# Half of a projection made early: the first layer's output product during the attention, for five token tiles instead of two

## The chip, the cores and the metric

The program runs on one core of a Trainium2 chip. The metric is the device time of one execution in microseconds (us), the median over runs. A core has a matrix engine (PE, with its weight loads shown as PEld), a vector engine (DVE), a scalar engine (ACT), a general engine (POOL) and a queue engine that issues the transfers (SP). Each engine takes its own instructions strictly in the order in which the program lists them, and waits at an instruction until what it needs is there.

## The reference, cut to what matters

The program is one inference step of a two-layer trunk over 640 token rows (512 latent rows and 128 prompt rows, five tiles of 128) of width 1024, in float32 accuracy. In the first layer one input projection feeds two kinds of heads, whose outputs stand side by side and go through one output projection:

```python
o_gla = rmsnorm(o_gla, g_gla) * jax.nn.silu(g_a.reshape(B, L, H_A, DV_A))      # 4 linear-attention heads: 512 columns
...
o_swa = banded_attn(q_b..., k_b, v_b, k_ctx, v_ctx, scale, sink_g)             # 8 windowed softmax heads: 512 columns
...
out = jnp.concatenate([o_gla.reshape(B, L, H_A * DV_A), o_swa.reshape(B, L, H_B * D_B)], axis=-1) @ w_out
```

Then, for each token row, `x = x + gate * rmsnorm(out, g)`, and the squared-ReLU network of the layer on `rmsnorm(x)` with a shift and a scale. The second layer (latent attention and a second network) is untouched here.

## The kernel before, in words

Every product keeps float32 accuracy by splitting each operand into a high and a low part: `mm3` (L136 to L140) issues three matmuls, high by high, high by low, low by high, into one accumulator. A weight tile of 128x1024 comes by DMA into one of three `raw` buffers; `split` casts its high part on ACT (L133) and subtracts on DVE (L134) into two tiles of the `ring`, which has 12 buffers (tag `w`, names `wt`, `q`, `kh`, `kl`, `Pr`, `PTr`).

The activations of all five tiles lie in `Hh` and `Hl` (high and low) as eight row blocks of 128. Blocks 0 to 3 are written by the linear attention (`gla_out`, L821), blocks 4 to 7 by the windowed softmax attention (`swa`, L932). The output projection of a tile is 8 blocks times 2 column halves times 3 matmuls, 48 matmuls of 128x512 into two accumulators `pso`.

The order of stages around the change is this. `gla_plan` finishes the products of the input projection and the linear attention. `swa` then runs eight heads for each of five tiles: `queries` transposes a tile's queries (`psq`) and splits them into `q`; `scores` copies the sink logit into the last column of a two-bank accumulator `pss` on ACT (L967) and makes the scores there (L970, L971, and the band mask L973); `soft_max` takes the row maximum on DVE (L979), `soft_exp` the exponential on ACT (L990), `soft_div` scales on POOL (L996); `trans` transposes the probabilities on PE (`pspt`, L1008) and copies them out as `PT` (L1009, by ACT and DVE in turn); `values` multiplies with the values into the accumulator `psov` (L1018), and `store` splits the result into `Hh` and `Hl`. `mod_steps` runs beside it: 96 matmuls `psmod` on 12 transfers of 1 MB (`mraw`), for the modulation vectors.

`out_ahead` (L497) makes blocks 0 to 3 of the output projection for the first `OA = 2` tiles while the attention runs, since these blocks are ready, and ACT copies each half into `acc` (L505). It gets the accumulator bank that the modulation holds until then; the other bank of that tag is `psov`. After the attention, `out_proj` (L508) makes blocks 4 to 7 for tiles 0 and 1 and adds to `acc` on DVE (L530), and all eight blocks for tiles 2 to 4 with a copy of the result (L532). `post` (L433) follows for each tile: a sum of squares on ACT (L309), two small POOL operations (L311, L312), a DVE scaling (L437), the residual add on POOL (on DVE for tile 4; L438) and its store; then `pre` (L319): again a sum of squares, the two POOL operations, a DVE scaling into `xn` (L324), eight transposes on PE (`pst`, L327), scale and shift by DVE and ACT (L335, L332), and the split into `Hh` (ACT, L339) and `Hl` (DVE L341, POOL through L130). `ff` (L536) starts with six feature blocks on tiles 0 and 1 ("part 0", matmuls `psf` of 128x256), then the same blocks on tiles 2 to 4 ("part 1", 128x384).

The code lists these steps in an order set by tables of planned times (`GLA_PLAN`, `SWA_PLAN`); a list scheduler then merges what it can for each engine by its own estimate of readiness and the priorities, so a change of the code can move instructions well away from the lines that it edits.

Of the kernel before, what the change touches and what calls it, by code (L numbers as in the profile page):

```python
# [11 lines left out]
F32 = mybir.dt.float32  # L12
# [31 lines left out]
OA = 2  # L44
# [52 lines left out]
def kernel(ctx: ExitStack, tc: tile.TileContext, I, O, dbg=None, stop=None):  # L97
# [390 lines left out]
    def out_weights(load, ks, alloc=None):  # L488
        wt = {}
        for k in ks:  # L490
            for n in range(2):
                hi, lo = wtile([P, 2, 512], lambda r: load(r, k, n), alloc if k == 6 else None)
                for i in range(2):
                    wt[k + i, n] = hi[:, i, :], lo[:, i, :]
        return wt

    def out_ahead(load, pp, acc, ts):  # L497

        wt = out_weights(load, (0, 2))
        for t in ts:  # L500
            for n in range(2):
# [3 lines left out]
                s.copy(out=acc[t][:, n * 512:(n + 1) * 512], in_=ps)  # L505
        return wt

    def out_proj(l, load, np_, pp, gate, accs, ahead=None):  # L508

        def alloc():  # L510
            return hid_tile(np_).rearrange("p a b -> p (a b)")

        begun = ()
        if ahead:
            wt, begun = ahead
        else:
            wt = out_weights(load, (0, 2))
        wt.update(out_weights(load, (4, 6), alloc))
        for t in range(NT):
            ts = slice(t * P, (t + 1) * P)  # L520
            pss = [pp.tile([P, 512], F32, tag="mm", name="pso") for _ in range(2)]
            k0 = 4 if t in begun else 0
            for k in range(k0, KD):
                for n in range(2):
                    mm3(pss[n], (Hh[:, k, ts], Hl[:, k, ts]), wt[k, n], k == k0, k == KD - 1)
            acc = begun[t] if k0 else accs(t)
            for n in range(2):
                c = slice(n * 512, n * 512 + 512)
                if k0:
                    v.tensor_tensor(out=acc[:, c], in0=pss[n], in1=acc[:, c], op=ALU.add)  # L530
# [62 lines left out]
    def mixer_ab(ap, bp, pa, pf, wf):  # L593
# [102 lines left out]
        qb = A["qb"] = bp.tile([P, NT, 512], F32, name="qb")  # L696
        gg = A["gg"] = ap.tile([P, NT, 512], F32, name="gg")
        ge = ap.tile([P, 512], F32, name="ge")
# [122 lines left out]
    def gla_out(A, p, pp, ap):  # L821
# [5 lines left out]
        for n0, nn in ((0, NS), (NS, 1)):  # L827
# [104 lines left out]
    def swa(A, pp, sp, ap, side):  # L932
# [29 lines left out]
        def scores(t, h):  # L962
# [4 lines left out]
            s.copy(out=ps[:, n:n + 1], in_=sink[:, h:h + 1])  # L967
            for o, k0, w in segs:
# [29 lines left out]
        def trans(t, kv, b):  # L998
# [5 lines left out]
            if (t, kv) not in EARLY:  # L1004
                PTs[t, kv][b] = sp.tile([P, 512], F32, tag="PT", name="PT", bufs=12)
# [486 lines left out]
    with pools(st=7, md=1) as ps:  # L1492
        with sb("start") as sp:
            pa, pf, wf = start(sp, ps)
        bp, ap = ms.enter_context(sb("bp")), gs.enter_context(sb("ap"))
        gp = gs.enter_context(sb("gp", "right"))
        A, products = mixer_ab(ap, bp, pa, pf, wf)
    with ms, pools(mm=2, gm=2, w2=2) as ps:
# [5 lines left out]
        def acc_tile(np_, t):  # L1504
            early = t < OA
            return (acp if early else np_).tile([P, D], F32, tag="acc", name="acc", bufs=OA if early else NT - OA)
        with sb("wa") as wa, sb("wp") as wp:
# [4 lines left out]
            begun = {t: acc_tile(None, t) for t in range(OA)}  # L1512
            ahead = out_ahead(load_w_out, ps, begun, range(OA)), begun
    with pools(mm=4, h=3, md=1) as ps:
        consts = mla_consts(dk, ps)
        with sb("fp") as fp:
            accs = lambda t: acc_tile(fp, t)
            out_proj(0, load_w_out, fp, ps, load_gate(0, 0, fp), accs, ahead)
# [3 lines left out]
            ff(0, fp, ps, lambda: load_gate(0, 1, fp), fp, accs,  # L1522
# [61 lines left out]
```

## Time and profile before

| what | value |
|---|---|
| runs | 1722.38, 1723.40 and 1726.54 us, median 1723.4 us |
| profiled execution | 1723.44 us, of which the span from first to last instruction is 1721.7 us |
| PE busy | 1652.6 us (96% of the span), mean granted clock 0.981 |
| DVE, ACT, POOL busy | 875.7, 682.4, 355.7 us |

The profiled execution lies 0.04 us from the median of the runs, and 1.7 us of it lie outside the span. In a list of instructions a row reads: start in us, length in us, engine, line, operation, output from inputs, shapes, count, and in brackets how long the engine stood idle before and what ended the wait. A PE row's length includes the drain of its pipeline, so back-to-back matmuls start closer together than their length.

### The profile page before, as it was taken

How to read it: one execution, taken by the hardware profiler on the slowest of the kernel's cores; microseconds unless marked ns; L12 is line 12 of the kernel's file. 1: busy time of each engine (PE TensorE's matmuls, PEld its weight loads, DVE VectorE, ACT ScalarE, POOL GpSimd, SP SyncE). 2: the span in 40 equal slices, each digit the busy share in tenths (PEclk: the TensorE clock that was granted, in tenths of full speed). 3: DMA queues.
4: the chain of work that ended last, by engine and by line, in shares of the span. 5: the costliest groups of instructions: out<-in, count | busy, mean ns of one | idle time of the engine just before them, and what ended most of it. 6: DMA issues, size and time to landing. Idle time of an engine off the chain costs nothing.

```text
span 1721.7 us, 25685 instructions
## 1 busy us (share of the span) xinstructions
PE 1652.6 (96%) x10270; PEld 1423.9 (83%) x10270; DVE 875.7 (51%) x1509; ACT 682.4 (40%) x1358; POOL 355.7 (21%) x422
## 2 busy tenths in 40 slices
PE   6989989999999999999999899999999999999997
PEld 5877775668998888889987788888889988999896
DVE  5368856546334343344476656566363344444443
ACT  4345345536341232132365565666353422232231
POOL 1135522233000000000163554443230000000003
PEclk9999989999999999999999999999999999999999
DMA  9311118156236465542231000112252321322212
GB/s 316 92 53 53 40 63 273 44 171 219 75 110 213 142 196 168 185 144 74 74 128 54 27 28 25 38 38 75 86 172 74 99 84 43 94 86 78 73 47 98
DMA packets 130933, 178.65 MB, mean 104 GB/s; under 512 B 7783, under 2 KB 95854, under 8 KB 129790
## 3 DMA queue, kind: packets, MB, share of 16 engines
q1 hardware_dynamic: 130814, 177.01, 32.6%
q8 instruction: 81, 1.33, 0.3%
q14 instruction: 38, 0.31, 0.1%
HBM read 165.93 MB, written 11.06 MB: 103 GB/s over the span
## 4 chain that ended last, share of the span: by engine, by line
PE 86%; DVE 6%; ACT 3%; DMA 2%; POOL 1%; issue 1%; SPq 0%; POOLq 0%; DVEq 0%; ACTq 0%
PE psf L138 9%; PE psf L139 9%; PE psf L140 9%; PE ps L138 8%; PE ps L139 8%; PE ps L140 8%; PE pso L1372 3%; PE psP L1350 3%; PE pso L138 2%; PE pso L139 2%; PE pso L140 2%; PE psmod L293 2%; PE pst L138 1%; PE psS L138 1%; PE psS L139 1%; PE psS L140 1%
## 5 line engine op out<-in xcount | busy, mean ns | idle before, releaser
L133 ACT CAST wt<-raw 128x1024 fp32r<-128x1024 f32 (+1 forms) x164 | 170.3, 1041 | 418.3 <-PE ps L139 240.7
L138 PE MATMUL psf<-Hh,wt 128*128 128x256 f32 (+1 forms) x1072 | 332.4, 311 | 1.2 <-ACT vt L656 1.2
L140 PE MATMUL psf<-Hh,wt 128*128 128x256 f32 (+1 forms) x1072 | 331.6, 309 | 0.0
L139 PE MATMUL psf<-Hl,wt 128*128 128x256 f32 (+1 forms) x1072 | 331.4, 309 | 0.0
L134 DVE TENSOR_TENSOR wt<-raw,wt 128x1024 fp32r<-128x1024 f32 (+1 forms) x164 | 207.4, 1267 | 224.7 <-ACT wt L133 206.5
L138 PE MATMUL ps<-wt,hid 128*128 128x512 f32 x640 | 250.3, 391 | 0.0
L139 PE MATMUL ps<-wt,hid 128*128 128x512 f32 x640 | 249.5, 390 | 0.0
L140 PE MATMUL ps<-wt,hid 128*128 128x512 f32 x640 | 249.2, 389 | 0.0
L138 PEld LDWEIGHTS psf<-Hh,wt 128*128 128x128 f32 x1072 | 203.3, 190 | 10.1 <-ACT hid L545 4.2
L311 POOL TENSOR_SCALAR ss<-ss 128x1 f32<-128x1 f32 x50 | 15.6, 312 | 943.8 <-ACT junk L309 943.1
L139 PEld LDWEIGHTS psf<-Hl,wt 128*128 128x128 f32 x1072 | 203.4, 190 | 1.4 <-issue 0.8
L140 PEld LDWEIGHTS psf<-Hh,wt 128*128 128x128 f32 x1072 | 203.5, 190 | 0.0
L583 DVE TENSOR_TENSOR acc<-ps,acc 128x512 f32<-128x512 f32 x120 | 82.3, 691 | 179.0 <-PE ps L140 178.9
L138 PEld LDWEIGHTS ps<-wt,hid 128*128 128x128 f32 x640 | 120.2, 188 | 32.0 <-ACT hid L545 4.2
L140 PEld LDWEIGHTS ps<-wt,hid 128*128 128x128 f32 x640 | 120.2, 188 | 25.0
L139 PEld LDWEIGHTS ps<-wt,hid 128*128 128x128 f32 x640 | 120.2, 188 | 24.3
L546 DVE TENSOR_TENSOR r<-r 128x384 f32<-128x384 f32 (+1 forms) x128 | 62.3, 488 | 110.0 <-ACT hid L545 109.9
L544 ACT ACTIVATE r<-psf 128x384 f32<-128x384 f32 (+1 forms) x128 | 55.6, 435 | 128.5 <-PE psf L140 128.5
L1339 POOL TENSOR_SCALAR Pm<-Pm,sm 128x768 f32<-128x768 f32 (+1 forms) x80 | 64.6, 810 | 117.9 <-DVE sm L1337 114.4
L1331 ACT ACTIVATE Pm<-psS,sm 128x768 f32<-128x768 f32 (+1 forms) x80 | 63.6, 796 | 26.8 <-PE psP L1350 15.8
L1319 DVE TENSOR_REDUCE sm<-psS 128x1 f32<-128x768 f32 x64 | 61.2, 956 | 21.4 <-PE psS L140 18.2
L1350 PE MATMUL psP<-ident,Pm 128*128 128x128 f32 x400 | 65.0, 280 | 0.0
(353 smaller groups left out, 3002.4 us busy)
## 6 DMA issues: line engine op xcount, KB each, us to landing
raw<-in_w_ff SPq DMA_DIRECT2D x128, 512.0 KB
mraw<-in_w_mod SPq DMA_DIRECT2D x60, 512.0 KB
mraw<-in_w_mod SPq DMA_DIRECT2D x18, 1024.0 KB
raw<-in_w_in_ab SPq DMA_DIRECT2D x16, 512.0 KB
xdr<-xt SPq DMA_DIRECT2D x15, 512.0 KB
xt<-xdr SPq DMA_DIRECT2D x15, 512.0 KB
xt<-in_x_sample SPq DMA_DIRECT2D x8, 512.0 KB
gate<-gdr SPq DMA_DIRECT2D x8, 512.0 KB
```

The lines of the kernel that those rows point to most:

```text
L133: s.copy(out=hi, in_=src)
L134: sub(out=lo, in0=src, in1=f32(hi), op=ALU.subtract)
L138: pe.matmul(out, lhsT=ah, rhs=bh, start=first, stop=False)
L139: pe.matmul(out, lhsT=ah, rhs=bl, start=False, stop=False)
L140: pe.matmul(out, lhsT=al, rhs=bh, start=False, stop=last)
L544: s.activation(out=r[:, 0:n], in_=ps, func=ACTF.Relu)
L546: v.tensor_tensor(out=r[:, 0:n], in0=r[:, 0:n], in1=r[:, 0:n], op=ALU.mult)
L583: v.tensor_tensor(out=acc[t][:, ns], in0=pss[n], in1=acc[t][:, ns], op=ALU.add)
L1319: v.tensor_reduce(out=st[:, 0, 0:1], in_=ps[:, 0:768], axis=AX.X, op=ALU.max, negate=True)
L1331: s.activation(out=Pm[:, c], in_=ps[:, c], func=ACTF.Exp, bias=st[:, 0, x:x + 1], accum_out=st[:, 1, x:x + 1])
L1339: g.tensor_scalar(Pm[:, c], Pm[:, c], st[:, 1, x:x + 1], 1.0, op0=ALU.mult, op1=ALU.mult)
L1350: pe.transpose(pt[:, (b - a) * P:(b - a + 1) * P], Pm[:, b * P:(b + 1) * P], ident)
```

## The change

All five tiles get blocks 0 to 3 of the output projection during the attention, one column half after the other: first the left halves of tiles 0 to 4, then the right halves. `out_proj` then makes only blocks 4 to 7, and adds to `acc` for every tile. The accumulators of tiles 2 to 4 take the buffers in which the queries of the attention lay (a pool `qa` of three buffers, each of which holds the queries of two tiles first), so the accumulator of tile 2 is free after the queries of tile 1 are transposed, that of tile 3 after tile 3's, that of tile 4 after tile 4's. Smaller edits come with it: the sink logit is copied into `pss` after the score matmuls instead of before; the gate of the linear attention is computed in place in `gg` (the scratch tile `ge` goes); `gla_out` takes its two heads in the order 1, 0 in some loops; `PT` has 11 buffers instead of 12; and the weights of blocks 6 and 7 lie in the ring instead of in `hid`.

```diff
-    def out_ahead(load, pp, acc, ts):
-
-        wt = out_weights(load, (0, 2))
-        for t in ts:
-            for n in range(2):
+    def out_ahead(load, pp, acc):
+
+        for n in range(2):
+            wt = out_weights(load, (0, 2), (n,))
+            for t in range(NT):
                 ps = pp.tile([P, 512], F32, tag="mm", name="pso")
                 for k in range(4):
                     mm3(ps, (Hh[:, k, t * P:(t + 1) * P], Hl[:, k, t * P:(t + 1) * P]), wt[k, n], k == 0, k == 3)
                 s.copy(out=acc[t][:, n * 512:(n + 1) * 512], in_=ps)
...
-        begun = ()
-        if ahead:
-            wt, begun = ahead
-        else:
-            wt = out_weights(load, (0, 2))
-        wt.update(out_weights(load, (4, 6), alloc))
+        k0, wt = (4, out_weights(load, (4, 6))) if begun else (0, {**out_weights(load, (0, 2)), **out_weights(load, (4, 6), alloc=alloc)})
...
-        qb = A["qb"] = bp.tile([P, NT, 512], F32, name="qb")
+        qbs = [qa.tile([P, D], F32, tag="qa", name="qb", bufs=3) for _ in range(3)]
+        qb = A["qb"] = [qbs[t // 2][:, t % 2 * 512:t % 2 * 512 + 512] for t in range(NT)]
...
             ps = pp.tile([P, 1024], F32, tag="w2", name="pss")
-            s.copy(out=ps[:, n:n + 1], in_=sink[:, h:h + 1])
             for o, k0, w in segs:
...
+            s.copy(out=ps[:, n:n + 1], in_=sink[:, h:h + 1])
...
-                PTs[t, kv][b] = sp.tile([P, 512], F32, tag="PT", name="PT", bufs=12)
+                PTs[t, kv][b] = sp.tile([P, 512], F32, tag="PT", name="PT", bufs=11)
...
-        def acc_tile(np_, t):
-            early = t < OA
-            return (acp if early else np_).tile([P, D], F32, tag="acc", name="acc", bufs=OA if early else NT - OA)
+        def acc_tile(t):
+            return acp.tile([P, D], F32, tag="acc", name="acc", bufs=2) if t < 2 else qa.tile([P, D], F32, tag="qa", name="acc", bufs=3)
...
-            begun = {t: acc_tile(None, t) for t in range(OA)}
-            ahead = out_ahead(load_w_out, ps, begun, range(OA)), begun
+            begun = [acc_tile(t) for t in range(NT)]
+            out_ahead(load_w_out, ps, begun)
```

No engine gets more or less work, but for six copies of `pso` to `acc` more on ACT during the attention, and six adds in place of six copies after it. What changes is the order. The line numbers of the change are lower than those of before: L504 there is L505 here, L966 is L967, L137 to L139 are L138 to L140.

The first place is ACT near the end of the attention (tile 4's queries `q`, the exponentials `Pm`, the stores `Hh` of the attention). Before:

```order
182 L505 COPY acc<-pso 128x512
183 L133 CAST Hh<-psov 128x4x128
184 L1009 COPY PT<-pspt 128x512
185 L959 ACTIVATE q<-psq 64x4x128
186 L990 ACTIVATE Pm,sm<-pss,sm 128x513
187 L1009 COPY PT<-pspt 128x512
188 L967 COPY pss<-sink 128x1
189 L959 ACTIVATE q<-psq 64x4x128
190 L967 COPY pss<-sink 128x1
191 L990 ACTIVATE Pm,sm<-pss,sm 128x513
192 L990 ACTIVATE Pm,sm<-pss,sm 128x129
```

With the change:

```order
177 L132 CAST Hh<-psov 128x4x128
178 L1002 COPY PT<-pspt 128x512
179 L966 COPY pss<-sink 128x1
180 L952 ACTIVATE q<-psq 64x4x128
181 L983 ACTIVATE Pm,sm<-pss,sm 128x513
182 L132 CAST wt<-raw 128x1024
183 L952 ACTIVATE q<-psq 64x4x128
184 L132 CAST wt<-raw 128x1024
185 L504 COPY acc<-pso 128x512
186 L1002 COPY PT<-pspt 128x512
187 L966 COPY pss<-sink 128x1 x2
188 L983 ACTIVATE Pm,sm<-pss,sm 128x513
```

Before, the row 182 is the last `acc` copy of the attention. With the change, four such copies stand before row 177 as before, and six more come from row 185 on, between exponentials, with two weight casts ahead of the first of them.

The second place is PE at the start of the windowed attention (`psq` the transposes of tile 0's queries, `pso` here the outputs of the linear attention, `pss` the scores). Before:

```order
704 L835 MATMUL pso<-va,AT 128x128 x4
705 L842 MATMUL pso<-sf_644,qh 128x128
706 L842 MATMUL pso<-st,qh 128x128 x6
707 L842 MATMUL pso<-sb_645,qh 128x128
708 L953 MATMUL psq<-ident,qb 128x128 x2
709 L835 MATMUL pso<-va,AT 128x128 x4
710 L842 MATMUL pso<-sf_644,qh 128x128
711 L842 MATMUL pso<-st,qh 128x128 x6
712 L842 MATMUL pso<-sb_645,qh 128x128
713 L953 MATMUL psq<-ident,qb 128x128 x2
714 L970 MATMUL pss<-kh,q 128x256
```

With the change:

```order
704 L946 MATMUL psq<-ident,qb 128x128 x4
705 L828 MATMUL pso<-va,AT 128x128 x4
706 L835 MATMUL pso<-sf_647,qh 128x128
707 L835 MATMUL pso<-st,qh 128x128 x6
708 L828 MATMUL pso<-va,AT 128x128 x4
709 L835 MATMUL pso<-sf_647,qh 128x128
710 L835 MATMUL pso<-st,qh 128x128 x6
711 L835 MATMUL pso<-sb_648,qh 128x128 x2
712 L962 MATMUL pss<-kh,q 128x256
```

The four transposes now stand ahead of the linear attention's outputs, and ACT makes `q` from them ahead of that attention's sums of squares; three heads of scores follow where one did.

The third place is ACT after the output projection (`junk` the sums of squares, of `acc` in `post` and of `xt` in `pre`; `r` and `hid` the results of the network's part 0). Before, from the sum of squares of tile 3's `acc`:

```order
223 L309 ACTIVATE junk,ss<-acc 128x1024
224 L133 CAST wt<-raw 128x1024 x3
225 L332 ACTIVATE hf<-pst,modT_85,gm_2801 128x128 x4
226 L309 ACTIVATE junk,ss<-xt 128x1024
227 L339 CAST Hh<-hf 128x4x128 x2
228 L133 CAST wt<-raw 128x1024 x2
229 L532 COPY acc<-pso 128x512
230 L309 ACTIVATE junk,ss<-acc 128x1024
```

With the change, from the same operation:

```order
222 L308 ACTIVATE junk,ss<-acc 128x1024
223 L132 CAST wt<-raw 128x1024
224 L331 ACTIVATE hf<-pst,modT_85,gm_2805 128x128 x4
225 L338 CAST Hh<-hf 128x4x128 x2
226 L536 ACTIVATE r<-psf 128x256
227 L537 ACTIVATE hid<-r 128x256
228 L536 ACTIVATE r<-psf 128x256
229 L537 ACTIVATE hid<-r 128x256
230 L308 ACTIVATE junk,ss<-xt 128x1024
231 L308 ACTIVATE junk,ss<-acc 128x1024
```

The sums of squares of tile 3's `xt` and of tile 4's `acc` now stand behind the results of the first two feature blocks of part 0. On PE the transposes `pst` of tile 4 stood among part 0 and now stand behind all of its 144 matmuls.

More of the change, by code (lines that the diff above doesn't have):

```diff
@@ L43 @@
 PVP = 150
-OA = 2
 QR = 1
@@ L486, in hid_tile, with out_weights @@
         return np_.tile([P, 2, T], R, tag="hid", name="hid", bufs=6)
-    def out_weights(load, ks, alloc=None):
+    def out_weights(load, ks, ns=(0, 1), alloc=None):
         wt = {}
         for k in ks:
-            for n in range(2):
+            for n in ns:
                 hi, lo = wtile([P, 2, 512], lambda r: load(r, k, n), alloc if k == 6 else None)
@@ L495, in out_weights @@
         return wt
-    def out_ahead(load, pp, acc, ts):
-        wt = out_weights(load, (0, 2))
-        for t in ts:
-            for n in range(2):
+    def out_ahead(load, pp, acc):
+        for n in range(2):
+            wt = out_weights(load, (0, 2), (n,))
+            for t in range(NT):
                 ps = pp.tile([P, 512], F32, tag="mm", name="pso")
@@ L505, in out_ahead, with out_proj @@
                 s.copy(out=acc[t][:, n * 512:(n + 1) * 512], in_=ps)
-        return wt
-    def out_proj(l, load, np_, pp, gate, accs, ahead=None):
+    def out_proj(l, load, np_, pp, gate, accs, begun=None):
         def alloc():
             return hid_tile(np_).rearrange("p a b -> p (a b)")
-        begun = ()
-        if ahead:
-            wt, begun = ahead
-        else:
-            wt = out_weights(load, (0, 2))
-        wt.update(out_weights(load, (4, 6), alloc))
+        k0, wt = (4, out_weights(load, (4, 6))) if begun else (0, {**out_weights(load, (0, 2)), **out_weights(load, (4, 6), alloc=alloc)})
         for t in range(NT):
@@ L590, in ff, with mixer_ab @@
             f0 += nf
-    def mixer_ab(ap, bp, pa, pf, wf):
+    def mixer_ab(ap, bp, qa, pa, pf, wf):
         w_in = I["w_in_ab"][0]
@@ L704, in use_q @@
             if t < NS:
-                rope_tok(qb[:, t, :], ps, t, 8, bp)
+                rope_tok(qb[t], ps, t, 8, bp)
             else:
-                s.copy(out=qb[:, t, :], in_=ps)
+                s.copy(out=qb[t], in_=ps)
         def use_g(t, ps):
+            ge = gg[:, t, :]
             s.activation(out=ge, in_=ps, func=ACTF.Exp, scale=-1.0)
@@ L712, in use_g @@
             s.activation(out=ge, in_=ge, func=ACTF.Exp, scale=-1.0)
-            v.tensor_tensor(out=gg[:, t, :], in0=ps, in1=ge, op=ALU.mult)
+            v.tensor_tensor(out=ge, in0=ps, in1=ge, op=ALU.mult)
         def use_b(a, c0, c1, ps, f=0):
@@ L833, in gla_out @@
             for n in range(n0, n0 + nn):
-                for r in range(2):
+                for r in ((1, 0) if nn > 1 else (0, 1)):
                     pe.matmul(ov(r, n), lhsT=AT[:, r, n, :], rhs=va[:, n, (2 * p + r) * P:(2 * p + r + 1) * P],
@@ L839, in gla_out @@
                 for d in range(2):
-                    for r in range(2):
+                    for r in (1, 0):
                         rs = slice(r * 64, r * 64 + 64)
@@ L952, in queries @@
             for x in range(4):
-                pe.transpose(ps[:, x, :], qb[:, t, x * P:(x + 1) * P], ident)
+                pe.transpose(ps[:, x, :], qb[t][:, x * P:(x + 1) * P], ident)
             q = (ring.tile([P, 1024], R, tag="w", name="q").rearrange("p (h n) -> p h n", h=HB) if t < QR
@@ L1516 @@
         with sb("fp") as fp:
-            accs = lambda t: acc_tile(fp, t)
-            out_proj(0, load_w_out, fp, ps, load_gate(0, 0, fp), accs, ahead)
+            out_proj(0, load_w_out, fp, ps, load_gate(0, 0, fp), acc_tile, begun)
             dump(h1h=f32(Hh), h1l=f32(Hl))
```

7 lines of the change are left out of this document (3 added, 4 removed).

## The prediction, made before the change was timed

> **What bounds the kernel now.** I read the page first, for the engine that bounds:
>
> ```profile
> span 1721.7 us, 25685 instructions
> PE 86%; DVE 6%; ACT 3%; DMA 2%; POOL 1%; issue 1%; SPq 0%; POOLq 0%; DVEq 0%; ACTq 0%
> ```
>
> 86% of the chain that ends last is PE, so a moved matmul gains nothing by itself: it must land where PE stood idle or slow. I then cut the stages around the change into windows (start and end, length, then busy time of PE, its weight loads, DVE, ACT, POOL, the clock granted to PE, the share of the transfers, GB/s):
>
> ```profile
> 220.00:230.00 10.00, 7.01 (x55) 6.25 (x53) 2.03 (x4) 4.62 (x21) 2.16 (x3) 0.89 0.03 8
> 307.90:329.60 21.70, 21.70 (x127) 16.24 (x126) 9.18 (x22) 9.21 (x27) 4.89 (x7) 1.00 0.10 25
> 329.60:354.60 25.00, 18.41 (x87) 10.69 (x87) 13.02 (x31) 11.87 (x39) 4.28 (x10) 0.78 0.15 43
> 354.60:403.00 48.40, 48.40 (x223) 40.15 (x224) 25.80 (x36) 24.02 (x43) 21.58 (x23) 0.97 0.51 168
> 403.00:423.40 20.40, 18.88 (x157) 18.47 (x156) 16.94 (x29) 13.21 (x29) 8.36 (x7) 1.00 0.88 297
> ```
>
> From 307.9 to 329.6 the four early units (12 matmuls each: one tile, one column half) fill PE completely. The 25.0 us behind them, the tail, hold nine heads (tile 3's last, tile 4's eight) with nothing to fill: PE is busy 18.41 us, at a clock of 0.78. Then come the output projection, 48.4 us of dense PE, and part 0 of the network, 20.4 us. The tail's lines, grouped, and its last rows on PE show what is late there:
>
> ```profile
> L1008 PE MATMUL pspt<-ident,Pm 128*128 128x128 f32 x36 | 8.0, 344 | 3.4 <-POOL Pm L996 2.1 <-DVE PT L1009 1.0
> L1018 PE MATMUL psov<-PT,vt 128*64 128x512 f32 x20 | 6.7, 811 | 0.8 <-DVE PT L1009 0.8
> ```
> ```profile
> 348.06 0.33 PE L970 MATMUL pss<-kh,q 128*128 128x128 f32 x1 [0.92 <-ACT pss L967]
> ...
> 351.32 0.48 PE L1008 MATMUL pspt<-ident,Pm 128*128 128x128 f32 x1 [1.53 <-POOL Pm L996]
> ...
> 352.58 1.98 PE L1018 MATMUL psov<-PT,vt 128*64 128x512 f32 x4 [0.78 <-DVE PT L1009]
> ```
>
> PE waits for the loop of a head: sink copy, maximum, exponential, division, transposes, copies. That is a wait which other matmuls can fill.
>
> **The change, part by part.**
>
> *Six units into the tail.* The price of a matmul is the distance of starts in a dense stretch:
>
> ```profile
> 358.81 0.39 PE L138 MATMUL pso<-wt,Hh 128*128 128x512 f32 x1
> ...
> 359.94 0.39 PE L140 MATMUL pso<-wt,Hl 128*128 128x512 f32 x1
> ...
> 417.19 1.09 PE L327 MATMUL pst<-ident,xn 128*128 128x128 f32 x8 [0.94 <-DVE xn L324]
> 418.04 0.37 PE L140 MATMUL psf<-Hh,wt 128*128 128x256 f32 x1
> 418.24 0.28 PE L138 MATMUL psf<-Hh,wt 128*128 128x256 f32 x1
> 418.36 0.28 PE L139 MATMUL psf<-Hl,wt 128*128 128x256 f32 x1
> ```
>
> The first two lie five starts apart: 1.13/5 = 0.226 us for 128x512. The last two give 0.12 us for 128x256; eight transposes take 418.04 − 417.19 = 0.85 us. The six moved units are 72 × 0.226 = 16.3 us. They leave the dense output projection, where they cost their full price. What they cost in the tail follows from the tail's own work at full clock. Upwards: 18.41 × 0.78 = 14.4 us, which counts drains as work. Downwards, by number: 36 transposes × 0.106 = 3.8, 20 of `psov` at 0.226 = 4.5, the remaining 18.41 − 8.0 − 6.7 = 3.7 us of scores and queries × 0.78 = 2.9; together 11.2. I take 13, so tail and units are 13 + 16.3 = 29.3 us of dense PE, more than the 25.0 that the heads' loop took. But the last head stands behind the last unit: from its score at 348.06 to 354.48 about 6.4 us passed, of which some 1.4 were matmuls; those 5 us of waits stay. The tail becomes 29.3 + 5 = **34 us**. The bounds are 29.3 (no wait left) and 25.0 + 16.3 = 41.3 (nothing filled). I lean to the side of the filled tail because of the window ahead of it: the same kind of unit, in the same one accumulator bank, held PE at 21.70 of 21.70 us. There a unit needs ACT's copy of the one before:
>
> ```profile
> 320.48 0.59 ACT L505 COPY acc<-pso 128x512 f32<-128x512 f32 x1 [1.33 <-PE pso L140]
> ```
>
> Six such copies more are 3.5 us on ACT, which is busy 11.87 of 25 us in the tail: beside PE, at nothing, unless a copy stands behind a blocked ACT (the slower rival).
>
> The Trainium skill speaks against this move: "TensorE: Matmul & The Clock Gate", section "A second HAM failure mode: psum-queue depth-cycling", says that a kernel which cycles accumulator banks leaves PE idle for short times between groups, so that its clock swings between half and full. By that the units would run at 0.78, as the tail does now, or less. The window 307.9 to 329.6 (clock 1.00, one bank, refilled four times) does not agree so far; the tail with units has no row here.
>
> *The way to part 1 on PE.* Part 1 begins with
>
> ```profile
> 423.26 0.52 PE L138 MATMUL psf<-Hh,wt 128*128 128x384 f32 x2
> ...
> 425.06 1.06 PE L293 MATMUL psmod<-mraw,cst 128*32 128x512 f32 x6
> ```
>
> and eight modulation matmuls (about 2 us) stand between its first; I count to 425.5. From 329.6 that is 25.0 + 48.4 + 20.4 + 2.1 = 95.9 us. With the change: 34 + 120 matmuls × 0.226 = 27.1, five tiles' transposes 4.3, part 0 of 144 × 0.12 = 17.2, modulation 2.1: 84.7 us, or **−11.2**. That assumes that the 3.9 us of holes which the stages now have beyond their count close; with them it would be −7.3.
>
> *The way to part 1 through ACT, DVE and POOL.* Behind the attention each tile needs two sums of squares on ACT with POOL and DVE steps between:
>
> ```profile
> 362.63 1.37 DVE L530 TENSOR_TENSOR acc<-pso,acc 128x512 f32<-128x512 f32 x2 [3.89 <-PE pso L140]
> ```
> ```profile
> 364.04 1.06 ACT L309 ACTIVATE junk<-acc 128x1024 bf16<-128x1024 f32 x1 [6.93 <-DVE acc L530]
> ...
> 371.22 1.06 ACT L309 ACTIVATE junk<-acc 128x1024 bf16<-128x1024 f32 x1
> ...
> 406.62 1.06 ACT L309 ACTIVATE junk<-acc 128x1024 bf16<-128x1024 f32 x1
> ```
> ```profile
> 367.61 2.40 POOL L130 TENSOR_TENSOR xt<-xt,acc 128x1024 f32<-128x1024 f32 x1 [1.45 <-PE pso L140]
> ```
>
> Tiles 2 to 4 get such adds (1.37/2 = 0.68 us on DVE) in place of ACT's copies of 0.59: nothing. ACT takes the squares in strict turn (`acc` of a tile, `xt` of the tile before), so two tiles cannot come closer than 371.22 − 364.04 = 7.2 us; the 2.40 us add on POOL is the long link. Now 48 matmuls per tile (10.8 us) hide that for tiles 2 to 4; with 24 (5.4 us) they don't, and this chain decides. After the change: attention's end 329.6 + 34 = 363.6; tile 0's 24 matmuls 5.4 and two adds 1.4, its square at 370.4; four tiles later 370.4 + 4 × 7.2 = 399.2, with a weight cast between 400. From tile 4's square to the equivalent start of part 1 the old kernel took 425.5 − 406.62 = 18.9, but 2.1 of that are the modulation matmuls, which can now run ahead of tile 4's transposes: 16.8 us, so part 1 stands at 417 against 425.5: **−8**. PE alone would be ready 3 us sooner; those are given back as a wait before tile 4's transposes.
>
> *The start of the attention.* Queries and three heads' scores move ahead of the linear attention's sums of squares on ACT. Today's hole:
>
> ```profile
> 229.85 0.58 PE L970 MATMUL pss<-kh,q 128*128 128x256 f32 x1 [2.99 <-DVE q L960]
> ```
> ```profile
> 298.82 5.31 DMA mraw<-in_w_mod
> ```
>
> The 2.99 us could go (PE is at 7.01 of 10 us there), but the chain passes through the last modulation transfer at 298.82, so most of what comes early waits there. Bounds −3 and 0; I take −1.
>
> *The rest.* The tail's sink copies, and the attention ahead of 307.9:
>
> ```profile
> L967 ACT COPY pss<-sink 128x1 f32<-128x1 f32 x9 | 1.4, 167 | 0.8 <-DVE q L960 0.8
> ```
> ```profile
> 262.00:307.90 45.90, 43.72 (x322) 27.11 (x321) 30.00 (x57) 24.80 (x61) 12.04 (x16) 1.00 0.77 260
> ```
>
> The copy behind the score matmuls: PE no longer waits for ACT (0.92 us above), ACT now waits for PE. Bounds: −7 us (all 40 copies of the row above off PE's way, 40 × 0.167) and +20 (the slower rival); taken at 0, since the score needs the same bank and the exponential the same maximum either way, and a third engine's step is only moved from before PE's to behind it. One buffer of `PT` less, `ge` in `gg`, the heads' order, weights in the ring instead of `hid`: cover is the work of dense stages such as that window (PE at 43.72 of 45.90 us), 0; if `PT` lacked cover it would cost a copy's wait such as the 0.78 us at 352.58 per tile, up to 4 us.
>
> **Sum.** −8 − 1 = −9 us from the profiled 1723.44 (span 1721.7 and 1.7 outside it), which is 0.04 from the median: 1714.4, said as **1714.5 us**.
>
> **The rivals.**
>
> *Better, 1709.5.* The last head's chain is filled too: tail 29.3 instead of 34, and the elementwise chain starts 5 us sooner with it. For it: the filler keeps PE dense from 307.9. Against it: the last score stands behind the last unit in PE's order, and nothing is left to fill with.
>
> *Given back, 1720 to 1723.* Two ways. First, DVE and POOL hold each other up in the shortened stage. The same operation twice:
>
> ```profile
> 395.51 4.56 DVE L134 TENSOR_TENSOR wt<-raw,wt 128x1024 fp32r<-128x1024 f32 x2
> ...
> 401.28 1.21 DVE L134 TENSOR_TENSOR wt<-raw,wt 128x1024 fp32r<-128x1024 f32 x1
> ```
> ```profile
> 388.05 1.30 POOL L130 TENSOR_TENSOR Hl<-hf,Hh 128x512 fp32r<-128x512 f32 x1 [0.47 <-ACT Hh L339]
> ...
> 411.21 4.29 POOL L130 TENSOR_TENSOR Hl<-hf,Hh 128x512 fp32r<-128x512 f32 x1 [2.49 <-ACT Hh L339]
> ```
>
> A POOL subtraction grows by 3.0 us where DVE is busy. If the last two tiles meet that on the chain, +6: 1720.5. The Trainium skill, "SBUF — State Buffer", section "🔬 SBUF: two separate sides", says that a DVE operation with two inputs in SBUF and a POOL operation that reads SBUF exclude each other for a whole instruction; these rows agree in direction. Second, the clock stays low in the tail: 29.3/0.78 = 37.6, + 5 = 42.6 instead of 34, so +8.6: 1723.
>
> *Slower, about 1734.* ACT takes its instructions in order. A sink copy that waits for score matmuls behind a unit of 12 × 0.226 = 2.7 us blocks the exponentials, query copies and `acc` copies behind it, and PE waits for these. All 40 heads of the attention have such a copy. At 0.5 us each (a score's two or three matmuls) that is 20 us: −9 + 20 = +11. It decides from (9 + 5.2)/40 = 0.36 us per head. For it: PE's waits in the tail are for ACT and what follows it. Against it: from 262 to 307.9 PE has other work to fill its waits (43.72 of 45.90), and ACT is busy only 24.80.
>
> **How the numbers follow.** 0.3% is 5.2 us, about what tells a difference from none here. Forecast, 1711 to 1718, 0.45; better 0.17; given back 0.25 (0.17 contention, 0.08 clock); slower 0.13. Faster by more than 0.3% is the first two, 0.62; within it 0.25; slower 0.13. The range, 1707 to 1726, holds the better case with 2.5 us for the attention's start, and the given-back case with some `PT` waits; it leaves out the slower rival and a few hundredths below.
>
> **What will show it.** In the changed trace: from the end of tile 2's `psov` to the end of tile 4's, 34 us with a clock near 1.00 (41 and more, or 0.8, speaks for the clock or ACT); behind it 120 `pso` matmuls; ACT's `junk` rows of `acc` 7.2 us apart rather than 10.8; PE waiting for `xn` of tile 4 for about 3 us before part 1; part 1 some 8 us nearer to tile 2's `psov` end than now. Sink copies with long idle time before them, released by PE, with PE waiting for `pss` on ACT's exponential, would show the slower rival; `Hl` and `wt` rows of 3 to 5 us in the last tiles the contention. I would be wrong at the root if the attention before 307.9, dense now, grew holes.

## The result and the profile after

The changed kernel takes **1733.1 us** (1731.4 to 1734.0 over 6 runs) against 1723.2 us: a ratio of 1.0051, 95% interval [1.0038, 1.0064] (8.8 us by the ratio over all runs, 9.9 between the medians). It is slower by 0.5%, where 1714.5 us, 9 us faster, was forecast; the time lies outside the range.

The page of the changed kernel, whose profiled execution has a span 7.9 us longer:

```profile
span 1729.6 us, 25696 instructions
PE 85%; DVE 6%; ACT 3%; DMA 2%; POOL 2%; issue 2%; POOLq 0%; SPq 0%; ACTq 0%; DVEq 0%
```

The stages of both, from 180 us on, cut at the same events: the end of the input projection's last products, the first transposes `pspt` of the windowed attention, the end of tile 2's `psov`, and for the change also the end of tile 4's, the end of the output projection and the start of part 1. (Columns as before: start and end, length, busy time of PE, its weight loads, DVE, ACT, POOL, the clock, the share of the transfers, GB/s.) Before:

```profile
180.00:220.40 40.40, 38.15 (x259) 30.15 (x258) 33.30 (x60) 9.71 (x10) 20.67 (x15) 1.00 0.07 23
220.40:251.40 31.00, 23.88 (x159) 21.70 (x158) 15.88 (x42) 15.78 (x66) 10.70 (x14) 0.78 0.14 49
251.40:329.60 78.20, 75.00 (x509) 50.65 (x510) 45.75 (x91) 41.25 (x105) 19.59 (x26) 0.98 0.56 190
```

After:

```profile
180.00:222.80 42.80, 38.25 (x234) 30.12 (x233) 34.71 (x56) 10.96 (x11) 19.21 (x14) 1.00 0.13 39
222.80:255.30 32.50, 24.15 (x159) 21.74 (x157) 14.94 (x40) 15.59 (x66) 10.71 (x14) 0.81 0.10 34
255.30:334.90 79.60, 75.22 (x509) 51.35 (x509) 46.10 (x91) 41.50 (x104) 20.54 (x26) 0.97 0.57 191
334.90:370.90 36.00, 30.21 (x161) 21.79 (x159) 18.33 (x35) 19.70 (x50) 4.31 (x10) 0.98 0.31 82
370.90:401.20 30.30, 30.24 (x139) 24.69 (x137) 16.20 (x22) 12.15 (x23) 12.74 (x14) 0.97 0.51 181
401.20:435.10 33.90, 25.84 (x180) 23.50 (x180) 27.15 (x44) 20.62 (x44) 16.12 (x16) 0.85 0.58 194
```

Three things stand in these rows. The first three stages, in which PE's busy time is nearly the same, take 2.4, 1.5 and 1.4 us longer: 5.3 us are lost before the tail begins. (One trace is one execution. In the ten traces of this document in which PE's order up to the tail is that of the kernel before, tile 2's `psov` ends between 327.2 and 332.9 us; so what the late start costs is read from the timed runs e2 and e3, not from these rows.) The tail is 36.0 us, close to the 34 forecast, at a clock of 0.98. And part 0, with its 144 matmuls and three tiles' transposes (17.2 + 2.6 us at the prices of the prediction), lasts 33.9 us, with PE busy only 25.84 of them. Its largest hole is one wait, for tile 2:

```profile
407.76 1.94 PE L326 MATMUL pst<-ident,xn 128*128 128x128 f32 x8 [6.62 <-DVE xn L323]
```

From the attention's end to the first matmul of the network's second product (two events that all kernels have) the change takes 459.5 − 370.9 = 88.6 us, before 450.6 − 354.5 = 96.1: the 16.3 us of matmuls taken out of this stretch shortened it by 7.5 us only. With +11.1 us in the tail and +5.3 ahead of it that is +8.9 us; the rest of the program gives 1.0 back.

**Ahead of the attention.** PE waits near the end of the input projection for weights of the query product that DVE subtracts later than before. At the start of the windowed attention it waits for the exponential `Pr`, which frees the accumulator of the third head's scores, and later for DVE's gate products `gy` and `gyp`:

```profile
186.89 0.50 PE L138 MATMUL pst<-wt,Hh 128*128 128x512 f32 x1 [1.14 <-DVE wt L133]
191.80 0.50 PE L138 MATMUL pst<-wt,Hh 128*128 128x512 f32 x1 [1.89 <-DVE wt L133]
...
233.78 0.58 PE L962 MATMUL pss<-kh,q 128*128 128x256 f32 x1 [3.36 <-ACT Pr L983]
...
249.09 1.25 PE L852 MATMUL psyt<-ident,gy 128*128 128x128 f32 x4 [2.44 <-DVE gy L850]
...
253.96 0.71 PE L852 MATMUL psyt<-ident,gyp 128*128 128x128 f32 x2 [1.91 <-DVE gyp L850]
```

The wait at 233.78 goes back to DVE's row maxima, which wait for the sink copies on ACT, which stand behind the linear attention's sums of squares. The `gy` of the wait at 249.09 needs POOL's `rs`, made from the next such sums:

```profile
232.22 1.29 DVE L972 TENSOR_REDUCE sm<-pss 128x1 f32<-128x513 f32 x2 [6.10 <-ACT pss L966]
...
248.68 2.16 DVE L850 SCALAR_TENSOR_TENSOR gy<-pso,rs,gg 128x128 f32<-128x128 f32 x8 [0.66 <-POOL rs L846]
```

The kernel before has waits in this stage too (2.99 us at 229.85, then 1.74, 1.64 and 0.76, where the change has 3.36, 2.44, 1.91 and 0.68), so the stage is only 1.5 us longer.

**Behind the attention.** ACT's sums of squares of `acc`, tiles 0 to 4, and in the fourth and sixth row `xt` of tiles 2 and 3:

```profile
378.39 1.06 ACT L308 ACTIVATE junk<-acc 128x1024 bf16<-128x1024 f32 x1 [6.82 <-DVE acc L522]
...
385.52 1.06 ACT L308 ACTIVATE junk<-acc 128x1024 bf16<-128x1024 f32 x1
...
394.28 1.06 ACT L308 ACTIVATE junk<-acc 128x1024 bf16<-128x1024 f32 x1
...
401.60 1.06 ACT L308 ACTIVATE junk<-xt 128x1024 bf16<-128x1024 f32 x1 [0.52 <-POOL xt L129]
...
405.62 1.05 ACT L308 ACTIVATE junk<-acc 128x1024 bf16<-128x1024 f32 x1
...
418.26 1.04 ACT L308 ACTIVATE junk<-xt 128x1024 bf16<-128x1024 f32 x1
...
419.43 1.06 ACT L308 ACTIVATE junk<-acc 128x1024 bf16<-128x1024 f32 x1
```

The tiles follow each other after 7.1, 8.8, 11.3 and 13.8 us, not 7.2 each: 41.0 us instead of 28.8. What lies between them from tile 1 on are the weight splits and the later steps of the tiles ahead, on DVE and POOL at once:

```profile
396.35 1.29 POOL L129 TENSOR_TENSOR Hl<-hf,Hh 128x512 fp32r<-128x512 f32 x1
398.81 2.76 POOL L129 TENSOR_TENSOR xt<-xt,acc 128x1024 f32<-128x1024 f32 x1 [1.16 <-DVE acc L436]
...
411.83 2.89 POOL L129 TENSOR_TENSOR Hl<-hf,Hh 128x512 fp32r<-128x512 f32 x1 [2.65 <-ACT Hh L338]
414.68 2.39 POOL L129 TENSOR_TENSOR xt<-xt,acc 128x1024 f32<-128x1024 f32 x1
```
```profile
363.31 2.58 DVE L133 TENSOR_TENSOR wt<-raw,wt 128x1024 fp32r<-128x1024 f32 x2 [1.70 <-ACT wt L132]
...
388.01 1.28 DVE L436 SCALAR_TENSOR_TENSOR acc<-acc,rs,gate 128x1024 f32<-128x1024 f32 x1 [0.76 <-POOL rs L311]
...
396.41 2.31 DVE L436 SCALAR_TENSOR_TENSOR acc<-acc,rs,gate 128x1024 f32<-128x1024 f32 x1 [0.47 <-POOL rs L311]
399.25 4.53 DVE L133 TENSOR_TENSOR wt<-raw,wt 128x1024 fp32r<-128x1024 f32 x2
```

The sums themselves were ready long before:

```profile
394.66 1.28 DVE L522 TENSOR_TENSOR acc<-pso,acc 128x512 f32<-128x512 f32 x2
...
404.99 1.27 DVE L522 TENSOR_TENSOR acc<-pso,acc 128x512 f32<-128x512 f32 x2
```

Tile 3's `acc` was complete at 395.9 and was squared at 405.62, tile 4's at 406.3 and at 419.43. Tile 3's residual add (414.68) stands behind tile 2's low part (411.83) on POOL; ACT's square of tile 3's `xt` (418.26) needs that add, which ended at 417.07, and then stands 1.2 us more behind part 0's results `r` (417.53) and `hid` (417.94); tile 4's square stands behind that one.

The kernel before had nearly the same spacing: its five squares of `acc` go from 364.04 to 406.62, 42.6 us, hidden there behind PE's 48 matmuls for each of tiles 2 to 4. Taking 16.3 us of matmuls away left 41.0 of it.

### The profile page after: what moved, and what is told of

Its sections match the earlier page's. It is cut to its first block, busy times and chain, and to the rows that moved or that the text cites. A ratio compares the mean times of both kernels' runs of the same rounds, so it can differ in the third digit from the quotient of the medians.

```text
span 1729.6 us, 25696 instructions
## 1 busy us (share of the span) xinstructions
PE 1650.8 (95%) x10270; PEld 1423.7 (82%) x10270; DVE 883.2 (51%) x1512; ACT 684.9 (40%) x1361; POOL 358.5 (21%) x422
## 3 DMA queue, kind: packets, MB, share of 16 engines
q1 hardware_dynamic: 130814, 177.01, 32.3%
## 4 chain that ended last, share of the span: by engine, by line
PE 85%; DVE 6%; ACT 3%; DMA 2%; POOL 2%; issue 2%; POOLq 0%; SPq 0%; ACTq 0%; DVEq 0%
PE psf L137 9%; PE psf L138 9%; PE psf L139 9%; PE ps L137 8%; PE ps L138 8%; PE ps L139 8%; PE pso L1365 3%; PE psP L1343 3%; PE pso L137 2%; PE pso L138 2%; PE pso L139 2%; PE psmod L292 2%; PE psS L137 1%; PE psS L138 1%; PE psS L139 1%
## 5 line engine op out<-in xcount | busy, mean ns | idle before, releaser
L137 PE MATMUL psf<-Hh,wt 128*128 128x256 f32 (+1 forms) x1072 | 332.2, 311 | 2.3 <-ACT vt L648 1.2
L138 PE MATMUL psf<-Hl,wt 128*128 128x256 f32 (+1 forms) x1072 | 331.4, 309 | 0.4 <-POOL Hl L129 0.4
L139 PE MATMUL psf<-Hh,wt 128*128 128x256 f32 (+1 forms) x1072 | 331.3, 309 | 0.0
L137 PE MATMUL ps<-wt,hid 128*128 128x512 f32 x640 | 250.3, 391 | 0.0
L138 PE MATMUL ps<-wt,hid 128*128 128x512 f32 x640 | 249.5, 390 | 0.0
L139 PE MATMUL ps<-wt,hid 128*128 128x512 f32 x640 | 249.2, 389 | 0.0
L137 PEld LDWEIGHTS psf<-Hh,wt 128*128 128x128 f32 x1072 | 203.7, 190 | 11.3 <-ACT hid L537 3.4
L138 PEld LDWEIGHTS psf<-Hl,wt 128*128 128x128 f32 x1072 | 203.8, 190 | 1.2 <-POOL Hl L129 0.7
L139 PEld LDWEIGHTS psf<-Hh,wt 128*128 128x128 f32 x1072 | 203.7, 190 | 0.0
L137 PEld LDWEIGHTS ps<-wt,hid 128*128 128x128 f32 x640 | 120.2, 188 | 32.0 <-ACT hid L537 4.2
L139 PEld LDWEIGHTS ps<-wt,hid 128*128 128x128 f32 x640 | 120.2, 188 | 25.2
L138 PEld LDWEIGHTS ps<-wt,hid 128*128 128x128 f32 x640 | 120.2, 188 | 24.2
```

Of the source, the lines that this page charges most:

```text
L137: pe.matmul(out, lhsT=ah, rhs=bh, start=first, stop=False)
L138: pe.matmul(out, lhsT=ah, rhs=bl, start=False, stop=False)
L139: pe.matmul(out, lhsT=al, rhs=bh, start=False, stop=last)
```

## The experiments

The theory after the trace: the move itself is worth a little; two small edits (gate in place, sink copy behind the scores) cost about 5 us at the start and some in the tail; and the chain through ACT, DVE and POOL behind the attention gives most of the move back. All ratios are to the kernel before on the same chip in the same series.

| run | ahead | gate, sink | other | tail, us | attention's end to second product, us (modulation matmuls in it) | ratio [95%] |
|---|---|---|---|---|---|---|
| before | 2 | old | | 24.9 | 96.1 (8) | 1 |
| the change | 5 | new | | 36.0 | 88.6 (8) | 1.0051 [1.0038, 1.0064] |
| e1 | 5 | old | | 31.7 | 88.7 (8) | 0.9991 [0.9981, 1.0000] |
| e2 | 5 | gate old | | 35.4 | 88.8 (8) | 1.0014 [1.0003, 1.0024] |
| e3 | 2 | gate new | | 24.6 | 95.7 (8) | 1.0029 [1.0019, 1.0039] |
| e4 | 2 | sink new | | 26.3 | 96.6 (8) | 1.0007 [0.9998, 1.0017] |
| e5 | 3 | old | | 24.9 | 99.7 (24) | 0.9995 [0.9982, 1.0007] |
| e6 | 4 | old | | 29.2 | 90.7 (20) | 1.0003 [0.9994, 1.0012] |
| e7 | 5 | old | adds on DVE | 31.7 | 87.6 (24) | 0.9981 [0.9972, 0.9990] |
| e8 | 5 | old | low parts on DVE | 32.3 | 88.2 (20) | 1.0000 [0.9991, 1.0008] |
| e9 | 5 | old | adds on DVE, modulation later | 32.5 | 82.6 (0) | 0.9959 [0.9945, 0.9974] |
| e10 | 4 | old | as e9 | 29.2 | 86.3 (0) | 0.9978 [0.9967, 0.9988] |
| e11 | 3 | old | as e9 | 24.9 | 87.6 (0) | 0.9953 [0.9935, 0.9971] |
| e12 | 2 | old | adds on DVE | 24.8 | 97.4 (24) | 1.0004 [0.9994, 1.0014] |

The tail is counted from the end of tile 2's `psov` to the end of tile 4's. A modulation matmul that runs ahead of the second product is one fewer later.

### e1: the move alone

```diff
+        ge = qbs[2][:, 512:1024]
...
-            ge = gg[:, t, :]
...
-            v.tensor_tensor(out=ge, in0=ps, in1=ge, op=ALU.mult)
+            v.tensor_tensor(out=gg[:, t, :], in0=ps, in1=ge, op=ALU.mult)
...
             ps = pp.tile([P, 1024], F32, tag="w2", name="pss")
+            s.copy(out=ps[:, n:n + 1], in_=sink[:, h:h + 1])
             for o, k0, w in segs:
...
-            s.copy(out=ps[:, n:n + 1], in_=sink[:, h:h + 1])
```

> The changed kernel with two small edits undone: the gate gets a scratch of its own again (the unused half of the third query buffer), and the sink copy stands before the score matmuls. The six moved units stay. Its order equals that of before up to the tail. Theory (the late start of the attention, 5.3 us at the end of tile 2's values, comes from these two edits): tile 2's values end near 329.6 as before, time 1733.1 - 5.3 = about 1728. Rival (the start is late because of the query buffers or the weights of the units): still about 335 there, and 1733. In both, from the attention's end to part 1 about 63 us stay.

Measured: 1720.7 us against 1722.0, 0.9991. The start came back, and more than that: the tail fell from 36.0 to 31.7 us, which was not expected. The window, and the wait of the last head's transposes in it, here and (second fence) in the change:

```profile
327.70:359.40 31.70, 29.58 (x161) 21.82 (x159) 17.58 (x35) 19.23 (x49) 5.28 (x10) 1.00 0.25 69
```
```profile
357.27 0.33 PE L1001 MATMUL pspt<-ident,Pm 128*128 128x128 f32 x1 [0.93 <-POOL Pm L989]
```
```profile
363.62 0.22 PE L962 MATMUL pss<-kh,q 128*128 128x128 f32 x1
...
368.00 0.33 PE L1001 MATMUL pspt<-ident,Pm 128*128 128x128 f32 x1 [3.81 <-POOL Pm L989]
```

With the sink copy behind the scores, the last head's score stands behind the last unit on PE, and its copy on ACT behind an `acc` copy; a weight cast stands between copy and exponential:

```profile
364.54 0.58 ACT L504 COPY acc<-pso 128x512 f32<-128x512 f32 x1
365.01 0.17 ACT L966 COPY pss<-sink 128x1 f32<-128x1 f32 x1
365.11 1.04 ACT L132 CAST wt<-raw 128x1024 fp32r<-128x1024 f32 x1
366.13 0.37 ACT L983 ACTIVATE Pm<-pss,sm 128x129 f32<-128x129 f32 x1
```

With the copy in front, the list scheduler puts that score ahead of the unit. Behind the attention nothing changed: 88.7 us, with the same hole, 6.64 us, before tile 2's transposes. So the move alone gains about 1.5 us by the ratio, with 1.0000 at the end of the interval; in the trace the tail is 6.8 us longer and the way behind it 7.4 shorter.

### e2 and e3: the gate in place

e2 is the change with only the first three pieces of the diff above; e3 is the kernel before with the opposite edit.

> The changed kernel with only the gate's scratch given back; the sink copy stays behind the score matmuls. Theory: the order before the first scores is that of before, so some 3.5 to 4 of the 5.3 us come back, 1729 to 1730; the rest is the sink copy's. Rival (the sink copy costs all of it by blocking ACT): 1733, and tile 2's values still end near 335.

> The kernel before with one edit of the change: the gate computed in place. Theory: the linear attention ends some 2.5 us later and the first transposes of the attention 4 us later, and nothing gives that back: 1723.4 + 4 = about 1727. Rival (the wait for the last modulation transfer hides a late start, or the edit is neutral): 1723 to 1724.

Measured: e2 1724.4 us, 1.0014; e3 1727.3 us, 1.0029, against 1722.0. The gate in place costs 0.0029, 5.0 us, in the kernel before, and (1.0051 − 1.0014) 6.4 us in the change: against an expected 4, which lies within e3's noise (0.0019 is 3.3 us); e2 came 5 us under its 1729 to 1730. The rival "hidden" is out. e3's trace shows the two waits of the change at the same places:

```profile
186.59 0.50 PE L139 MATMUL pst<-wt,Hh 128*128 128x512 f32 x1 [1.16 <-DVE wt L134]
191.50 0.50 PE L139 MATMUL pst<-wt,Hh 128*128 128x512 f32 x1 [1.90 <-DVE wt L134]
```

The arithmetic of the gate is the same. What the edit took away is one buffer that the next token tile had to wait for (1.39 us on ACT at 153.68 in the kernel before, for DVE's `gg`); without it, the list scheduler moved the gate's steps and, with them, the states and weight subtractions on DVE. Whether the writing in place has a cost of its own, beside the new order, was not separated: no run gave the gate a second scratch buffer, which would change the order without writing in place.

### e4: the sink copy behind the scores, alone

```diff
             ps = pp.tile([P, 1024], F32, tag="w2", name="pss")
-            s.copy(out=ps[:, n:n + 1], in_=sink[:, h:h + 1])
...
+            s.copy(out=ps[:, n:n + 1], in_=sink[:, h:h + 1])
             Ss[t, h] = ps, n
```

> The kernel before with one edit of the change: the sink copy behind the score matmuls. Theory (a small loss at the start of the attention, where PE has nothing else): +1 to +2, 1725. Rival of the prediction (40 copies block ACT at 0.5 us each): +10 to +20, 1733 to 1743. Second rival (PE's wait for ACT goes): -1 to -4, 1720 to 1722.

Measured: 1723.8 us, 1.0007 [0.9998, 1.0017]: +1.2 us, not clear of zero and no more than the tail alone is longer (26.3 against 24.9). The prediction's slower rival at 0.5 us per head is refuted; over 40 heads it is 0.03. But with five tiles ahead the same edit costs (1.0014 − 0.9991) 4.0 us, of which 3.7 lie in the tail (35.4 against 31.7): its price depends on what stands in ACT's and PE's queues, and the change put units there.

### e5 and e6: three and four tiles ahead

The kernel before with `OA = 3` and `OA = 4`, `acc` of tile 2 and on in the query buffers, sink copy and gate as before. (The change's query buffers, its order of the heads and its 11 buffers of `PT` stay in; up to the tail PE's order is that of the kernel before, matmul for matmul.)

```diff
-OA = 2
+OA = 3
...
-            begun = {t: acc_tile(None, t) for t in range(OA)}
+            begun = {t: acc_tile(t) for t in range(OA)}
```

> The kernel before with three tiles ahead instead of two (tile by tile, as before; gate's scratch and sink copy as before): two units more in the tail. The first run gave a tail of 31.7 us with six units more against 25.0 with none, 1.1 us per unit against a price of 2.7 us. Theory (elementwise chain of 62.7 us from the attention's end to part 1 is the floor, PE decides above it): tail 27.2, PE's way behind it 70.9 - 5.4 = 65.5, which is above the floor: -3.2 us, ratio 0.998. Rival (what units save behind the attention is always given back): ratio 1.000.

> As the run with three tiles, with four tiles ahead, four units more in the tail. Theory of the floor: tail 29.5; PE's way behind it 70.9 - 10.9 = 60.0 is below the floor, so 62.7: -3.7 us, ratio 0.998, about the same as three tiles and 2 us better than five (1.5 us). Rival (PE decides all the way, no floor): 29.5 + 60.0 = -6.4 us, ratio 0.996.

Measured: 1721.7 and 1722.8 us against 1722.8: 0.9995 and 1.0003. Neither gain of 0.002 was there. The tails were 24.9 and 29.2 us: two more units cost nothing at all (2.3 us were expected), four cost 4.3. In e5's trace a wait stands at the head of part 1 that had not been in any list:

```profile
426.62 1.94 PE L293 MATMUL psmod<-mraw,cst 128*32 128x512 f32 x8 [3.37 <-DMA mraw<-in_w_mod]
```

These are the matmuls of the next modulation step. The list scheduler places them where it takes PE to be idle; their weights come into buffers that `xt`, `xn` and `hf` of the last tiles still hold (the transfers' queue waited 4.2 us there for DVE's `xn`). This trace is of the slowest of e5's 12 runs, 5.8 us over their median, so the wait's length in the others is not known. For four tiles no such wait shows; the profiled span is 2.7 us shorter than that of before, but that execution lies 1.9 us under the median of its own runs, and the timed runs show no gain; what held it back stays open.

### e7 and e8: the chain through ACT, DVE and POOL

e1 with the residual adds of this layer's mixer on DVE for all tiles (e7), or with the low parts of blocks 0 to 3 on DVE (e8):

```diff
-        (gpair if t < NS else v.tensor_tensor)(out=xt, in0=xt, in1=src, op=ALU.add)
+        (gpair if t < NS and (l or w) else v.tensor_tensor)(out=xt, in0=xt, in1=src, op=ALU.add)
```
```diff
-        gpair(Hl[:, 0:4, ts], f[:, 0:4], f32(Hh[:, 0:4, ts]), ALU.subtract)
+        (gpair if l or not half else v.tensor_tensor)(out=Hl[:, 0:4, ts], in0=f[:, 0:4], in1=f32(Hh[:, 0:4, ts]), op=ALU.subtract)
```

> Five tiles ahead, gate's scratch and sink copy as before (as in the first run), and the residual add of the first layer's mixer on DVE for all tiles instead of POOL for tiles 0 to 3 (1.22 against 2.40 us). Theory (chain through ACT, DVE and POOL is the floor, and POOL's adds and DVE's splits hold each other up): the way from the attention's end to part 1 falls from 62.7 by 4 to 7 us, time -5 to -8 us to before, ratio 0.996. Rival (the floor is ACT's queue, or DVE, which gets the work): 62 to 64 us, ratio 0.999 to 1.000.

> Five tiles ahead, gate's scratch and sink copy as before, and in the split behind the first layer's mixer the low parts of blocks 0 to 3 on DVE (0.69 us) instead of POOL (1.3 to 4.3 us); the residual add stays on POOL. Theory: the way from the attention's end to part 1 falls by 1 to 4 us, less than with the adds, since only the last tiles' low parts stand on the chain: ratio 0.997 to 0.999. Rival (DVE is the floor): unchanged or longer, ratio 0.999 to 1.001.

Measured: e7 1719.0 us, 0.9981 (0.996 expected: half of it came); e8 1721.7 us, 1.0000 (0.997 to 0.999 expected), against 1722.8. e7's five squares of `acc`, first and last:

```profile
370.08 1.06 ACT L308 ACTIVATE junk<-acc 128x1024 bf16<-128x1024 f32 x1 [6.66 <-DVE acc L522]
...
401.70 1.06 ACT L308 ACTIVATE junk<-acc 128x1024 bf16<-128x1024 f32 x1
```

31.6 us, where e1 took 40.1 and the change 41.0: with the four adds off POOL the chain is 8.5 us shorter, and part 1 could have begun near 415, 52 us after the attention's end instead of 63. But there the modulation matmuls wait again:

```profile
415.39 1.07 PE L292 MATMUL psmod<-mraw,cst 128*32 128x512 f32 x8
420.66 2.67 PE L292 MATMUL psmod<-mraw,cst 128*32 128x512 f32 x12 [4.21 <-DMA mraw<-in_w_mod]
```

On SP's queue those transfers stand behind tile 4's store:

```profile
409.54 0.33 SPq L438 DMA_DIRECT2D xdr<-xt  x1
409.96 16.40 SPq L280 DMA_DIRECT2D mraw<-in_w_mod  x10
```

e8 shows no gain in time, as its rival had it, although its squares span 38.0 us, 2.1 less than e1's; whether DVE is the reason, as the rival says, was not shown.

### e9 to e12: the modulation matmuls moved out of the way

The accumulator of the next modulation step comes from the tag of the network's products, so that the list scheduler places its matmuls behind part 1 (at 497 us and later in e9):

```diff
-            return pp.tile([P, 512], F32, tag="md", name=name)
+            return pp.tile([P, 512], F32, tag="mm" if l == 0 and name == "psmod" else "md", name=name)
```

e9 is e7 with it, e10 and e11 are e6 and e5 with it and the adds on DVE; e12 is the kernel before with the adds alone.

> As the run with five tiles ahead and the adds on DVE (ratio 0.9981, in whose trace PE waited 4.21 us at the head of part 1 for a modulation transfer), and the accumulator of the next modulation step now comes from the bank tag that the network's products use, so that these matmuls stand behind part 1 on PE. Theory (that transfer, which needs the buffers of tile 4's chain, took the gain of the shorter chain): the 4.2 us go, about -7.5 us to before, ratio 0.9956. Rival (something else is late at the same place): 0.998.

> Four tiles ahead, adds on DVE, modulation matmuls behind part 1. Theory: tail 29.2 as measured with four tiles (+4.3 to before), PE's way behind it -10.9, and the chain through ACT, DVE and POOL, now some 53 us, no longer decides: -6.6 us, ratio 0.996. Rival (the chain still decides at 62 to 63 us): -3 us, ratio 0.998.

> Three tiles ahead, adds on DVE, modulation matmuls behind part 1. Theory: tail 24.9 as measured with three tiles (+0.1), PE's way behind it -5.4, nothing waits: -5.3 us, ratio 0.997, and the transfer wait of 3.4 us that the run with three tiles had is gone. Rival (that wait was no cost): ratio 0.9995 as there.

> Control: the kernel before with only the adds of the first layer's mixer on DVE. Theory (with 48 matmuls for each of tiles 2 to 4 the chain lies hidden behind PE; only the holes of 0.6 and 0.9 us before the last two tiles' transposes could go): ratio 0.999 to 1.000. Rival (the adds alone make the gain of the run with five tiles): 0.998.

Measured: e9 1714.9 us, 0.9959 (0.9956 expected); e10 1719.1, 0.9978 (0.996 expected, outside its interval; its rival's 0.998 is inside); e11 1714.8, 0.9953 (0.997 expected, at the end of its interval); e12 1722.0, 1.0004, all against 1722.0. Only the place of those matmuls differs between e9 and e7: the wait of 4.21 us is gone, and 3.8 us (0.0022) came, though the two intervals just touch. The traces show less of it: from the end of tile 2's `psov` to the last instruction e7 takes 1385.9 us and e9 1385.0; that the transfer wait cost as much as 3.8 us rests on the timed runs alone. e7 itself is not clear of e1 (0.9981 against 0.9991, the intervals overlap), but both edits together, e9, are. e12 shows that the adds alone bring nothing measurable while PE has 48 matmuls per tile to do. In e9 part 1 now waits for the chain's own end:

```profile
415.27 1.00 PE L137 MATMUL psf<-Hh,wt 128*128 128x384 f32 x4 [2.69 <-ACT Hh L338]
```

e11 reaches with three tiles what e9 reaches with five, since its tail is free. Both beat the kernel before by 7 to 8 us; their intervals overlap, so the two are not ranked. e10's way behind the attention, 86.3 us, misses the 85.2 (96.1 − 10.9) of its theory although no modulation matmul (1 us for eight) is left in it: there too part 1 waits, 2.64 us, for the chain.

## Why the prediction was wrong, step by step

**Right.** The price of a unit: 120 matmuls and 16 transposes at the stated prices make 28.8 us, the output projection took 30.3. The tail: 29.3 us dense and 5 of waits were forecast, PE was busy 30.2 of 36.0. That 36.0 came so close to 34 is partly luck: with the sink copy in front the units filled most of those 5 us too (e1: 31.7), and the copy's place put 4 back. The clock: a rival let it stay at 0.78; it was 0.98 in the change and 1.00 in e1. The Trainium skill ("TensorE: Matmul & The Clock Gate", "A second HAM failure mode: psum-queue depth-cycling") tells of a kernel that cycles through accumulator banks and whose clock swings; the prediction carried that over to one refilled bank, and these traces, with 0.98 and 1.00, do not bear that out. That the chain through ACT, DVE and POOL decides behind the attention, not PE, and that a gain would end as a wait for `xn`: e1, e7, e9 and e12 together show it (in the change the wait came at tile 2, 6.6 us, not at tile 4, 3 us).

**Wrong, the chain's size.** The step is "four tiles later 370.4 + 4 × 7.2 = 399.2". The 7.2 came from tiles 0 and 1, the only pair between whose squares no other tile's steps lie. The change's squares span 41.0 us, 12.2 more; from the attention's end to the second product 78.5 us follow from the prediction (53.4 to part 1 and 25.1 for it) and 88.6 came: **+10**. The prediction took the wider spacing of the later tiles in its own rows (371.22 to 406.62, three times 11.8 us) for PE's 48 matmuls of 10.8 us each; with 24 it hardly shrank (385.52 to 419.43, three times 11.3), so the chain needs that much by itself. The prediction priced this as a rival (two low parts of 3.0 us, +6) instead of as part of the sum, though its own rows at 395.51 and 411.21 showed it. Moving the adds off POOL (e7) took 8.5 us off the chain; moving the low parts (e8) took 2.1 off and gained nothing in time, so the rival named the lesser operation. The rows agree with the Trainium skill ("SBUF — State Buffer", "🔬 SBUF: two separate sides"): two weight subtractions on DVE took 4.53 us beside POOL's add at 398.81, and 2.58 us at 363.31 with no POOL work beside them. How much of the 8.5 us is this hold-up, and how much the 1.2 us by which each of four adds is shorter on DVE, or the new order, was not separated.

**Wrong, the start.** The step is "I take −1" for the earlier queries and scores, with `ge` in `gg` among the edits "at 0". It was +5.3 us in the trace. The earlier queries, read as a gain, and the loss are one edit's doing: e3, whose only edit is the gate in place, has the four transposes ahead of the linear attention's outputs as the change has, and e2 and e3 put 5.0 to 6.4 us on it. I had read where the queries went, and not what DVE and ACT, in their new order, would reach later.

**Wrong, the sink copy.** "Taken at 0": 4.0 us in the change, 1.2, not clear of zero, in the kernel before. The slower rival named the mechanism, ACT in order behind PE's scores, and that its 1734 is near the time measured is luck: its size of 20 us is refuted, and the time is the sum of three other terms: chain +10, start +6 against the forecast, tail +2.

The sum: −9 + 10 + 6 + 2 = +9, and the trace has +8.9 at the second product. By the timed runs, the move alone gained 1.5 us (e1) where 8 were forecast, and the two small edits cost 6.4 and 4.0 us.

**Not seen at all**: the modulation transfers, the next wait after the chain (3.4 us in e5, 4.2 in e7). The prediction let these matmuls run ahead of tile 4's transposes without asking which buffers their weights need.

## What to carry to other kernels

When matmuls are moved out of a dense stage, that stage's other engines get less time for the same work: measure their chain over all tiles, with everything that shares their queues, not over the first pair, and then ask what is late next (here a transfer into buffers that the chain still holds). An edit that only saves a buffer can cost more than the move that it makes room for, since it takes away a wait that kept an order; undo such edits one by one. How many tiles to make ahead is a size to be tried: here three fit the tail's idle time without cost and five do not, though in time the two were not told apart.

## What the hardware showed that was not expected

One accumulator bank, emptied by copies of 0.58 us that start 3.7 to 7.5 us apart, went with a clock of 0.98 in the change's tail of 36.0 us and 1.00 in e1's of 31.7, where the same stage without the units ran at 0.78; with two and four units (e5, e6) it was 0.92. And a DVE scaling with two full-size operands took 2.31 us at 396.41, beside POOL's 1.29 us low part from 396.35 on, against 1.28 us at 388.01: the subtraction's slowdown is not peculiar to it.
